# One decode step of a hybrid trunk: building the S5 input table with tokens and channels on partitions

## The chip, the cores and the metric

One core of a Trainium2 chip runs the whole kernel. The metric is the device time of one execution in microseconds (us), the median of three; the profile is one further execution. TensorE does the matrix products, VectorE and ScalarE the elementwise work, Pool (GpSimd) and SyncE mostly issue DMAs.

## The reference

Two layers over 256 prompt tokens and 8 samples of 4 tokens, 288 token columns in all, width 2048. Layer 0 mixes by retention and RG-LRU, layer 1 by S5, a diagonal complex state space model with 128 groups of 16 channels and 64 states; an FFN of 5632 follows each. The change touches only what S5 needs of its weights:

```python
def s5(u, h0_re, h0_im, a_re, a_im, b_re, b_im, c_re, c_im, d, log_dt):
    dt = jnp.exp(log_dt.astype(f32))[:, None]
    mag = jnp.exp(a_re * dt)
    abr = mag * jnp.cos(a_im * dt)
    abi = mag * jnp.sin(a_im * dt)
    ...
    bbr = fr[..., None] * b_re - fi[..., None] * b_im
    bbi = fr[..., None] * b_im + fi[..., None] * b_re
    ...
        _, _, sr, si = lax.associative_scan(_cplx_combine, (abr_c, abi_c, bu_r, bu_i), axis=1)
        y = jnp.einsum('bcgp,gkp->bcgk', sr, c_re) - jnp.einsum('bcgp,gkp->bcgk', si, c_im)
```

Both kernels work through the tokens in blocks of CH = 4. For a block they need, per pair of groups (32 channels, 128 states; 64 pairs), the complex input weights times the powers 3, 2, 1, 0 of the transition (table P), the output weights times the powers 1 to 4 (table O), the 4 x 4 token-to-token products (table T), and rotations for the scan over blocks (table R).

## The kernel before

Every weight matrix is streamed from DRAM in halves of up to 8 tiles of 128 x 128. For each half SyncE issues the load (`raw`, four buffers), ScalarE rounds it to `wh` (L268, four buffers) and VectorE forms the rest `wl = raw - wh` (L96); each tile then takes three matmuls of 288 columns (L314 to L316), 24 for a half of 8 tiles. Two halves make a unit, whose sum `acc` (two buffers) VectorE evacuates: in gate and up units into `g`, with the activation behind it, in down units as a residual add into `X`. The order on every engine is written out by the program, with no scheduler. After each half `run_prog` counts a step on and calls `run_due`, which runs what is due and then one piece of the queue `bgq`. Ahead of half s it has issued `wl` up to half s + 2:

```python
                if c[2] >= done + (4 if hold else 3) or c[2] >= n or c[2] in hold:
                    break
                prepl_next()
```

so on VectorE the order is: `wl` of half s + 2, evacuation after half s (every second half), the piece of `bgq`, `wl` of half s + 3, and so on. VectorE works in this order; what waits holds up all behind it.

The tables are built in the FFN of layer 0 by pieces of `bgq`: `t1` and `t2` (constants, four instructions a piece), then eight chunks of eight pairs of groups (`table_chunk`), 23 pieces each: 7 for the rotations, 4 for `bstep` (complex products of 128 columns, states on partitions, and copies by ScalarE into `pst`), 6 for `cstep`, 4 for `tp` and 2 for `tt_`. A piece `tp` transposes four 128 x 128 blocks of `pst` on TensorE (L1244), ScalarE scales them into `stg` (L1249), and after each second piece Pool writes 512 KB to the DRAM table `tabP` (L1252). A piece `tt_` does eight token products of 32 x 128, an fp32 product in two passes (L1261), and writes `tabT` and `tabO` from Pool (L1267, L1270). The last piece, `s5_open`, closes the tables' buffers and issues the first loads of the finished tables from SyncE, on the queue that also loads the weights.

## Time and profile before

| | |
|---|---|
| median of three runs | 2535.65 us (2535.18 to 2535.86) |
| span of the profiled execution | 2533.9 us |
| TensorE busy | 2468.4 us, 97% |
| VectorE busy | 1592.1 us, 63% |
| ScalarE busy | 1152.4 us, 45% |
| Pool busy, DMA issue not counted | 104.7 us, 4% |
| DMA | 468.31 MB, 185 GB/s in the mean |
| table build, first load to last table written | about 660 to 1265 us |

Busy time is the share of the span in which an engine had an instruction running. A wait in brackets is the idle time before an instruction and what ended it. Starts in a timeline count from the start of the span.

### The profile page before, as it was taken

To read this page: it belongs to the slowest core of one execution; us is meant where nothing else is said; L and a number is where in the kernel's file an instruction comes from. 1 tells how busy PE (TensorE), PEld (TensorE's weight loads), DVE (VectorE), ACT (ScalarE), POOL (GpSimd) and SP (SyncE) were. 2 spreads that over 40 slices of the span, in tenths; PEclk is the share of its full clock that TensorE was granted. 3 is DMA by queue.
4 is the path that set the end of the run, shared out by engine and by line. 5 is a ranking of instruction groups with operands and counts; after the bars stand their busy time and mean duration, and the time that the engine had idled before them with its cause. 6 is when DMAs were issued, how large, how long until landed. Compare 5 with 4: busy or idle time off the path is not lost.

```text
span 2533.9 us, 49270 instructions
## 1 busy us (share of the span) xinstructions
PE 2468.4 (97%) x20210; PEld 2428.2 (96%) x20210; DVE 1592.1 (63%) x2955; ACT 1152.4 (45%) x1786; POOL 104.7 (4%) x204
## 2 busy tenths in 40 slices
PE   8999999999999999999998789999999999999997
PEld 8899999999999999999997689999999999999997
DVE  7767666567766777667756975555544555445555
ACT  6646545433455655545533344443333333333342
POOL 0111110000000000000100000000000000000000
PEclk9999999999999999999999999999999999999999
DMA  7556645555566666666678855555455554445553
GB/s 251 181 173 193 203 151 181 164 166 167 182 217 198 209 199 207 212 210 196 204 239 250 277 163 165 167 164 166 164 163 173 166 164 161 161 163 166 167 163 125
DMA packets 155184, 468.31 MB, mean 185 GB/s; under 512 B 32912, under 2 KB 40976, under 8 KB 154960
## 3 DMA queue, kind: packets, MB, share of 16 engines
q1 hardware_dynamic: 140944, 421.16, 51.9%
q0 software_dynamic: 12288, 42.69, 4.6%
q8 instruction: 159, 2.61, 0.4%
q10 hardware_dynamic: 1728, 1.33, 0.2%
q14 instruction: 65, 0.53, 0.1%
HBM read 423.99 MB, written 41.11 MB: 184 GB/s over the span
## 4 chain that ended last, share of the span: by engine, by line
PE 92%; DVE 5%; DMA 2%; ACT 1%; issue 0%; SPq 0%; POOL 0%; DVEq 0%; ACTq 0%
PE acc L314 30%; PE acc L316 29%; PE acc L315 29%; DVE w L96 2%; DVE w L1421 1%; DMA raw<-in_w_in_dram 1%; PE mp L724 1%; PE mp L1244 1%; PE mp L776 0%; DVE Hs L96 0%; DVE g L105 0%; PE mp L1261 0%; PE mp L519 0%; DVE g L96 0%; DMA tab<-tabR 0%
## 5 line engine op out<-in xcount | busy, mean ns | idle before, releaser
L314 PE MATMUL acc<-xg,wh 128*128 128x288 f32 x3520 | 1047.9, 298 | 0.0
L268 ACT ACTIVATE wh<-raw 128x1024 fp32r<-128x1024 f32 (+1 forms) x736 | 758.9, 1035 | 426.2 <-PE acc L315 277.2
L316 PE MATMUL acc<-xg,wl 128*128 128x288 f32 x2816 | 829.0, 294 | 0.8 <-DVE wl L96 0.8
L315 PE MATMUL acc<-xg,wh 128*128 128x288 f32 x2608 | 765.5, 294 | 1.6 <-DVE xg L105 1.6
L96 DVE TENSOR_TENSOR wl<-raw,wh 128x1024 fp32r<-128x1024 f32 (+1 forms) x585 | 692.2, 1196 | 56.2 <-ACT wh L268 48.5
L314 PEld LDWEIGHTS acc<-xg,wh 128*128 128x128 f32 x3520 | 660.5, 188 | 3.0 <-issue 2.2
L314 PE MATMUL acc<-ac,wh 128*128 128x288 f32 x2064 | 613.5, 297 | 1.6 <-ACT ac L1479 1.0
L316 PEld LDWEIGHTS acc<-xg,wl 128*128 128x128 f32 x2816 | 529.2, 188 | 1.1 <-DVE wl L96 1.1
L315 PEld LDWEIGHTS acc<-xg,wh 128*128 128x128 f32 x2608 | 492.3, 189 | 2.5 <-DVE xg L105 2.0
L316 PE MATMUL acc<-ac,wl 128*128 128x288 f32 x1592 | 469.5, 295 | 0.7 <-DVE wl L96 0.7
L315 PE MATMUL acc<-ac,wh 128*128 128x288 f32 x1568 | 460.1, 293 | 0.0
L315 PE MATMUL acc<-x,wh 128*128 128x288 f32 x1408 | 415.4, 295 | 0.0
L314 PEld LDWEIGHTS acc<-ac,wh 128*128 128x128 f32 x2064 | 388.6, 188 | 4.7 <-issue 1.7
L96 DVE TENSOR_TENSOR g<-acc,rstd 128x288 f32<-128x288 f32 x192 | 87.6, 456 | 353.0 <-PE acc L316 352.5
L316 PEld LDWEIGHTS acc<-ac,wl 128*128 128x128 f32 x1592 | 300.0, 188 | 1.2 <-DVE wl L96 1.2
L315 PEld LDWEIGHTS acc<-ac,wh 128*128 128x128 f32 x1568 | 295.5, 188 | 0.0
L315 PEld LDWEIGHTS acc<-x,wh 128*128 128x128 f32 x1408 | 264.4, 188 | 0.1
L316 PE MATMUL acc<-xg,wlx 128*128 128x288 f32 x704 | 207.3, 294 | 0.0
L96 DVE TENSOR_TENSOR X<-X,acc 128x288 f32<-128x288 f32 x112 | 50.8, 454 | 243.2 <-PE acc L316 242.9
L96 DVE TENSOR_TENSOR wlx<-raw,wh 128x1024 fp32r<-128x1024 f32 (+1 forms) x151 | 179.4, 1188 | 6.8 <-ACT wh L268 6.8
L191 ACT ACTIVATE ac<-g 128x288 fp32r<-128x288 f32 x98 | 43.5, 444 | 286.9 <-DVE g L96 286.9
L316 PE MATMUL acc<-ac,wlx 128*128 128x288 f32 x472 | 139.2, 295 | 0.0
(279 smaller groups left out, 2030.3 us busy)
## 6 DMA issues: line engine op xcount, KB each, us to landing
raw<-in_w_gu_dram SPq DMA_DIRECT2D x352, 512.0 KB, 4.5
raw<-in_w_dn_dram SPq DMA_DIRECT2D x128, 448.0 KB, 4.1
raw<-in_w_in_dram SPq DMA_DIRECT2D x96, 512.0 KB, 4.5
raw<-in_w_dn_dram SPq DMA_DIRECT2D x64, 512.0 KB, 3.7
raw<-in_w_glu_dram SPq DMA_DIRECT2D x64, 512.0 KB, 4.7
raw<-in_w_out_dram SPq DMA_DIRECT2D x32, 512.0 KB, 4.4
out_ret_s_dram<-s POOLq DMA_DIRECT2D x16, 512.0 KB, 4.9
tabR<-R POOLq DMA_DIRECT2D x16, 512.0 KB, 6.8
```

What stands on the lines that cost most here:

```text
L96: v.tensor_tensor(o, a, b, op=op)
L191: act.activation(h, x, AF.Copy, scale=scale)
L268: act.activation(wh[:, :w], raws[i][:, :w], AF.Copy)
L314: pe.matmul(acc, lhsT=wh[:, o:o + P], rhs=xh, start=(k == u.k0), stop=False)
L315: pe.matmul(acc, lhsT=wh[:, o:o + P], rhs=xl, start=False, stop=False)
L316: pe.matmul(acc, lhsT=wl[:, o:o + P], rhs=xh, start=False, stop=(k == u.k1 - 1))
L724: pe.matmul(CR[h][32 * g:32 * g + 32, :256], lhsT=qm[:, dt, b2, :], rhs=t_[:, b2, dt, :], start=(c < 2 and dt == 0), stop=(c > 1 and dt == 1),
L1244: pe.transpose(ps[:, (2 * k + ri) * P:(2 * k + ri + 1) * P], st["ps"][:, ri, 4 * (jj // 2) + q].rearrange("p s i -> p (s i)"), ident)
L1421: v.tensor_tensor_scan(g[:, ri].rearrange("p q c -> p (q c)"), r4m, a[:, ri].rearrange("p q c -> p (q c)"), 0.0, op0=MUL, op1=ADD)
```

## The change

`t3` forms the input factor times the powers 0 to 3 for all groups in `s_wp` (states on partitions), `t4` transposes it in eight pieces and writes it to a new DRAM table `tabW`, 64 x 1024. A chunk then keeps one complex product of `bstep` (the power 0, for the token products). Table P is formed pair by pair with tokens and channels on partitions: for two pairs of groups (here called a pair, k = 0 to 3 in a chunk) `p_load` issues five DMAs from Pool, four that repeat a row of `tabW` over 32 partitions each (`pw`, 64 KB each) and one for the input weights, laid out ahead by the host (`pb`, 256 KB). `p_half` forms the real part in one piece and the imaginary part in the next, three VectorE operations of 256 columns each; the second of them also issues the next pair's loads, has ScalarE scale the result in place and Pool write 256 KB of `tabP`. `pw`, `pb` and `pout` have one buffer each. The sixteen token products of a chunk go into one PSUM bank in one piece. A chunk has 23 pieces as before: 7, 1, 6, 1 and 8.

```diff
     tabP = drp.tile([NT, P, 1024], F32, name="tabP")
     tabO = drp.tile([NT, P, 1024], F32, name="tabO")
     tabT = drp.tile([NT, P, P], F32, name="tabT")
+    tabW = drp.tile([64, CH, 2, P], F32, name="tabW")
     tabR = drp.tile([NT, P, 1024], F32, name="tabR")
...
-        later(10, lambda: (bgq.append(t1()), bgq.append(t2()), rest()))
+        wp = tb.tile([P, CH, 2, 64], F32, name="s_wp")
+
+        def t3():
+            for k, x in enumerate((fr, fi)):
+                v.tensor_copy(wp[:, 0, k], x)
+                yield 1
+            for e in range(1, CH):
+                pr, pi = wp[:, e - 1, 0], wp[:, e - 1, 1]
+                a, b, c, d = (g_(W) for _ in range(4))
+                tt(a, pr, abr, MUL)
+                yield 1
+                tt(b, pi, abi, MUL)
+                yield 1
+                tt(wp[:, e, 0], a, b, SUB)
+                yield 1
+                tt(c, pi, abr, MUL)
+                yield 1
+                tt(d, pr, abi, MUL)
+                yield 1
+                tt(wp[:, e, 1], c, d, ADD)
+                yield 1
+
+        def t4():
+            o = tb.tile([P, 2, 1024], F32, tag="R", name=nm("R"), bufs=1)[:64, 0]
+            for hf in range(2):
+                ps = mp_()
+                for k in range(4):
+                    pe.transpose(ps[:64, k * P:k * P + P], wp[:, 2 * hf + k // 2, k % 2], ident)
+                act.activation(o[:, 512 * hf:512 * hf + 512], ps[:64], AF.Copy)
+            pool.dma_start(tabW.rearrange("c e r n -> c (e r n)"), o)
+        later(10, lambda: (bgq.append(t1()), bgq.append(t2()), bgq.append(t3()), bgq.append(t4), rest()))
...
-            st["ps"] = tb.tile([P, 2, 8, CH, 32], F32, tag="ps", name=nm("pst"), bufs=1)
+            st["ps"] = tb.tile([P, 2, 8, 32], F32, tag="ps", name=nm("pst"), bufs=1)
...
-        def bput(e):
+        def bput():
             for ri in range(2):
-                put(st["ps"][:, ri, :, CH - 1 - e, :], st["w", e][ri], S["gm"])
+                put(st["ps"][:, ri], st["w"][ri], S["gm"])
...
-        def bstep(e):
-            def f():
-                if e == 0:
-                    b = st["bc"]
-                    st["w", 0] = cmul(bc(S["fr"]), bc(S["fi"]), b[:, :, 0], b[:, :, 1])
-                else:
-                    bput(e - 1)
-                    st["w", e] = cmul(bc(S["abr"]), bc(S["abi"]), *st["w", e - 1])
-            return f
+        def bstep():
+            b = st["bc"]
+            st["w"] = cmul(bc(S["fr"]), bc(S["fi"]), b[:, :, 0], b[:, :, 1])
...
-        def tp(jj):
+        def p_load(k):
+            c0 = 8 * ch + 2 * k
+            w = tb.tile([P, 2, 2, P], F32, tag="pw", name=nm("pw"), bufs=1)
+            b = tb.tile([P, 2, 2, P], F32, tag="pb", name=nm("pb"), bufs=1)
+            for s in range(CH):
+                pool.dma_start(w[32 * s:32 * s + 32], tabW[c0:c0 + 2, CH - 1 - s][None].to_broadcast([32, 2, 2, P]))
+            pool.dma_start(b, ins["ssm_bt"][:, c0:c0 + 2])
+            st["p", k] = w, b
+
+        def p_half(k, im):
             def f():
-                if jj % 2 == 0:
-                    st["stg"] = tb.tile([P, 4, 2, P], F32, tag="stg", name=nm("stg"), bufs=1)
-                ps = mp_()
-                for k in range(2):
-                    q = 2 * (jj % 2) + k
-                    for ri in range(2):
-                        pe.transpose(ps[:, (2 * k + ri) * P:(2 * k + ri + 1) * P],
-                                     st["ps"][:, ri, 4 * (jj // 2) + q].rearrange("p s i -> p (s i)"), ident)
-                for k in range(2):
-                    q = 2 * (jj % 2) + k
-                    c = 8 * ch + 4 * (jj // 2) + q
-                    act.activation(st["stg"][:, q].rearrange("p b c -> p (b c)"), ps[:, 256 * k:256 * k + 256],
-                                   AF.Copy, scale=S["g4"][:, c:c + 1])
-                if jj % 2:
-                    pool.dma_start(tabP[2 * ch + jj // 2], st["stg"].rearrange("p a b c -> p (a b c)"))
+                w, b = st["p", k]
+                if not im:
+                    st["po"] = tb.tile([P, 2, 2, P], F32, tag="po", name=nm("pout"), bufs=1)
+                x, y = (tb.tile([P, 2, P], F32, tag="px", name=nm("px"), bufs=2) for _ in range(2))
+                tt(x, w[:, :, 0], b[:, :, im], MUL)
+                tt(y, w[:, :, 1], b[:, :, 1 - im], MUL)
+                o = st["po"]
+                tt(o[:, :, im], x, y, ADD if im else SUB)
+                if im:
+                    if k < 3:
+                        p_load(k + 1)
+                    for q in range(2):
+                        c = 8 * ch + 2 * k + q
+                        act.activation(o[:, q], o[:, q], AF.Copy, scale=S["g4"][:, c:c + 1])
+                    pool.dma_start(tabP[c // 4][:, 512 * (k % 2):512 * (k % 2) + 512], o.rearrange("p q r n -> p (q r n)"))
             return f
 
-        def tt_(jj):
-            def f():
-                j = 2 * ch + jj
-                ps = mp_()
+        def tt_():
+            ps = mp_()
+            for jj in range(2):
                 for ri in range(2):
                     for q in range(4):
-                        pe.matmul(ps[32 * q:32 * q + 32, :P], lhsT=st["ps"][:, ri, 4 * jj + q, CH - 1, :],
+                        pe.matmul(ps[32 * q:32 * q + 32, P * jj:P * jj + P], lhsT=st["ps"][:, ri, 4 * jj + q, :],
                                   rhs=st["vz"][:, ri, 4 * jj + q, 0:CH, :].rearrange("p t o -> p (t o)"),
-                                  start=(ri == 0), stop=(ri == 1), tile_position=(0, 32 * q), skip_group_check=True)
+                                  start=(ri == 0 and jj == 0), stop=(ri == 1), tile_position=(0, 32 * q), skip_group_check=True)
+            for jj in range(2):
+                j = 2 * ch + jj
                 T = tb.tile([P, P], F32, tag="Tt", name=nm("Tt"), bufs=2)
-                act.activation(T, ps[:, :P], AF.Copy, scale=vec[:, V_ODD + j:V_ODD + j + 1])
+                act.activation(T, ps[:, P * jj:P * jj + P], AF.Copy, scale=vec[:, V_ODD + j:V_ODD + j + 1])
                 stt(T[:, :32], S["qm"], S["dg"][:, j:j + 1], T[:, :32], MUL, ADD)
                 pool.dma_start(tabT[j], T)
                 od = tabO[j].rearrange("p (q r n) -> p r q n", r=2, n=P)
                 for ri in range(2):
                     pool.dma_start(od[:, ri], st["vz"][:, ri, 4 * jj:4 * jj + 4, 1:CH + 1, :].rearrange("p q t o -> p q (t o)"))
-            return f
         def rview(c0, m0, m1):
...
-        for e in range(CH):
-            bgq.append(bstep(e))
+        bgq.append(bstep)
         for e in range(CH + 1):
             bgq.append(cstep(e))
-        bgq.append(lambda: cput(CH))
-        for jj in range(4):
-            bgq.append(tp(jj))
-        for jj in range(2):
-            bgq.append(tt_(jj))
+        bgq.append(lambda: (cput(CH), p_load(0)))
+        bgq.append(tt_)
+        for k in range(4):
+            bgq.append(p_half(k, 0))
+            bgq.append(p_half(k, 1))
...
+    bt = np.zeros((CH, 2, 16, 64, 2, 2, 64), np.float32)
+    for ri, k in enumerate(("ssm_b_re", "ssm_b_im")):
+        bg = a[k][0].reshape(64, 2, 64, 16).transpose(1, 3, 0, 2)
+        for g in range(2):
+            bt[:, g, :, :, ri, g, :] = bg[g]
+    o["ssm_bt"] = bt.reshape(P, 64, 2, P)
```

On Pool, from chunk 0's rotations (`tabR`) on, the queue before:

```order
L1303 DMA tabR<-R_7549 128x1024
L1252 DMA tabP<-stg_8249 128x1024 [waits Activation_49]
L1252 DMA tabP<-stg_8322 128x1024 [waits Activation_49]
L1267 DMA tabT<-Tt_8404 128x128 [waits DVE_49]
L1270 DMA tabO<-vzt_7548 512x1x128 x2
L1267 DMA tabT<-Tt_8449 128x128 [waits DVE_49]
L1270 DMA tabO<-vzt_7548 512x1x128 [waits DMASW2_49]
L1270 DMA tabO<-vzt_7548 512x1x128 [waits DMASW3_49]
```

and now, from the last token table of the chunk on (`DMASW` is the semaphore of a Pool DMA, `DMAHW` that of a SyncE DMA):

```order
L1305 DMA tabO<-vzt_7826 512x1x128 [waits DMASW6_49]
L1305 DMA tabO<-vzt_7826 512x1x128 [waits DMASW7_49]
L1266 DMA pw_8473<-tabW 32x2x256 [waits DMASW0_49,DVE_49]
L1266 DMA pw_8473<-tabW 32x2x256 [waits DMASW1_49]
L1266 DMA pw_8473<-tabW 32x2x256 [waits DMASW2_49]
L1266 DMA pw_8473<-tabW 32x2x256 [waits DMASW3_49]
L1267 DMA pb_8474<-in_ssm_bt_dram 128x512 [waits DMASW4_49]
L1286 DMA tabP<-pout_8435 128x512 [waits DMASW5_49,DVE_49,Activation_49]
L1266 DMA pw_8551<-tabW 32x2x256 [waits DMASW2_49,DMASW3_49,DMASW1_49,DMASW6_49,DMASW0_49,DVE_49]
```

Chunk 0's first loads (`pw_8342`, `pb_8343`) follow `tabR` directly and are not shown. The two large writes of `tabP` have become four smaller ones, and each but the last stands behind the five loads of the next pair, the first of which waits for VectorE.

On VectorE, in the same chunk, where the transposes and the token products stood, before:

```order
L96 TENSOR_TENSOR wl_117<-raw_8021,wh_8147 128x1024 [waits DMAHW3_49,Activation_49]
L96 TENSOR_TENSOR wl_115<-raw_8065,wh_8188 128x896 [waits DMAHW4_49,Activation_49]
L96 TENSOR_TENSOR X<-X,acc_8193 128x288 [waits PE_49]
L96 TENSOR_TENSOR wl_116<-raw_8106,wh_8222 128x1024 [waits DMAHW5_49,Activation_49]
L96 TENSOR_TENSOR wlx<-raw_8150,wh_8257 128x896 [waits DMAHW6_49,Activation_49]
L96 TENSOR_TENSOR X<-X,acc_8262 128x288 [waits PE_49]
L96 TENSOR_TENSOR wl_117<-raw_8191,wh_8295 128x1024 [waits DMAHW7_49,Activation_49]
L96 TENSOR_TENSOR wl_115<-raw_8225,wh_8330 128x896 [waits DMAHW0_49,Activation_49]
L96 TENSOR_TENSOR X<-X,acc_8335 128x288 [waits PE_49]
L105 SCALAR_TENSOR_TENSOR Tt_8404<-s_qm,s_dg,Tt_8404 128x32 [waits Activation_49]
```

and now:

```order
L96 TENSOR_TENSOR px_8468<-pw_8342,pb_8343 128x256 [waits DVE_49]
L96 TENSOR_TENSOR px_8469<-pw_8342,pb_8343 128x256
L96 TENSOR_TENSOR pout_8435<-px_8468,px_8469 128x2x128 [waits DVE_49]
L96 TENSOR_TENSOR wl_118<-raw_8311,wh_8441 128x1024 [waits DMAHW3_49,Activation_49]
L96 TENSOR_TENSOR px_8514<-pw_8473,pb_8474 128x256 [waits DMASW2_49,DMASW3_49,DMASW1_49,DMASW4_49,DMASW0_49,DVE_49]
L96 TENSOR_TENSOR px_8515<-pw_8473,pb_8474 128x256
L96 TENSOR_TENSOR pout_8513<-px_8514,px_8515 128x2x128 [waits DMASW5_49,DVE_49,Activation_49]
L96 TENSOR_TENSOR wl_116<-raw_8352,wh_8483 128x896 [waits DMAHW4_49,Activation_49]
L96 TENSOR_TENSOR X<-X,acc_8488 128x288 [waits PE_49]
L96 TENSOR_TENSOR px_8546<-pw_8473,pb_8474 128x256 [waits DVE_49]
```

Where only `wl` and `X` followed each other, each step now has three operations of a half, and the first half of the second pair waits for five Pool DMAs (its loads) and, at `pout`, for the write of the first pair.

On TensorE, one of the four places of a chunk where transposes stood between two halves, before:

```order
L315 MATMUL acc_8193<-ac_7927,wh_8103 128x288
L316 MATMUL acc_8193<-ac_7925,wlx 128x288
L1244 MATMUL mp_8250<-ident,pst_7547 128x128 x4
L314 MATMUL acc_8262<-ac_5814,wh_8147 128x288
L315 MATMUL acc_8262<-ac_5816,wh_8147 128x288
L316 MATMUL acc_8262<-ac_5814,wl_117 128x288
```

and the same chunk's token products now, where there were two groups of eight:

```order
L315 MATMUL acc_8313<-ac_7907,wh_8223 128x288
L316 MATMUL acc_8313<-ac_7905,wlx 128x288
L1294 MATMUL mp_8376<-vzt_7826,pst_7825 32x128 x16
L314 MATMUL acc_8410<-ac_5816,wh_8267 128x288
L315 MATMUL acc_8410<-ac_5818,wh_8267 128x288
L316 MATMUL acc_8410<-ac_5816,wl_118 128x288
```

The four transposes are gone from the chunk's first steps, and the sixteen products stand in one row of the queue.

## Rows read from the trace of the kernel before

**Rows 1.** The page: busy time by engine, and the chain's shares.

```profile
PE 2468.4 (97%) x20210; PEld 2428.2 (96%) x20210; DVE 1592.1 (63%) x2955; ACT 1152.4 (45%) x1786; POOL 104.7 (4%) x204
...
PE 92%; DVE 5%; DMA 2%; ACT 1%; issue 0%; SPq 0%; POOL 0%; DVEq 0%; ACTq 0%
```

**Rows 2.** Waits of TensorE: us in total, times, longest.

```profile
PE acc L316 <- DVE wl L96: 1.6, 3, 0.8
```

**Rows 3.** Stretches: us, each engine's busy time and instructions, PEclk, DMA share, GB/s.

```profile
600.00:620.00 20.00, 20.00 (x154) 20.00 (x153) 15.11 (x41) 7.38 (x9) 0.00 (x0) 1.00 0.46 149
...
1276.00:1286.00 10.00, 8.61 (x61) 7.91 (x61) 7.20 (x10) 5.84 (x8) 0.00 (x0) 1.00 0.64 198
...
1440.00:1460.00 20.00, 14.31 (x410) 12.59 (x402) 19.86 (x38) 9.01 (x23) 1.07 (x3) 0.86 0.91 266
```

**Rows 4.** Timeline (start us, us) of VectorE and SyncE near 1268.

```profile
1268.31 1.08 DVE L96 TENSOR_TENSOR wl<-raw,wh 128x896 fp32r<-128x896 f32 x1
1277.67 1.09 DVE L96 TENSOR_TENSOR wl<-raw,wh 128x896 fp32r<-128x896 f32 x1 [8.28 <-ACT wh L268]
...
1265.09 0.33 SPq L1356 DMA_DIRECT2D ss<-in_state_ssm_dram  x1
```

**Rows 5.** Timeline of TensorE around a group of transposes.

```profile
712.84 0.30 PE L316 MATMUL acc<-ac,wlx 128*128 128x288 f32 x1
712.98 0.60 PE L1244 MATMUL mp<-ident,pst 128*128 128x128 f32 x4
...
713.55 0.29 PE L315 MATMUL acc<-ac,wh 128*128 128x288 f32 x1
```

**Rows 6.** Groups by line: the transposes.

```profile
L1244 PE MATMUL mp<-ident,pst 128*128 128x128 f32 x128 | 19.2, 272 | 0.0
```

**Rows 7.** Timeline of TensorE around a group of token products.

```profile
726.60 0.29 PE L316 MATMUL acc<-ac,wlx 128*128 128x288 f32 x1
726.82 0.65 PE L1261 MATMUL mp<-vzt,pst 128*32 128x128 f32 x16
...
727.63 0.29 PE L315 MATMUL acc<-ac,wh 128*128 128x288 f32 x1
```

**Rows 8.** Timeline of VectorE: weights, 256-column operations, evacuation.

```profile
709.06 2.22 DVE L96 TENSOR_TENSOR wl<-raw,wh 128x1024 fp32r<-128x1024 f32 x2
...
749.07 1.42 DVE L96 TENSOR_TENSOR rt<-R,s_pw 128x256 f32<-128x256 f32 x4
750.41 0.75 DVE L96 TENSOR_TENSOR R<-rt,rt 128x256 f32<-128x256 f32 x2
...
803.24 0.46 DVE L96 TENSOR_TENSOR g<-acc,rstd 128x288 f32<-128x288 f32 x1 [1.42 <-PE acc L316]
...
805.44 0.25 DVE L105 SCALAR_TENSOR_TENSOR Tt<-s_qm,s_dg,Tt 128x32 f32<-128x32 f32 x1
```

**Rows 9.** Timeline of Pool: DMAs being issued.

```profile
729.02 1.51 POOL L1270 DMA_DIRECT2D tabO<-vzt  x2
...
753.89 1.09 POOL L1303 DMA_DIRECT2D tabR<-R  x2 [19.41 <-ACT wh L268]
```

**Rows 10.** DMA issues: times, KB each, median us to landing.

```profile
...
tabP<-stg POOLq DMA_DIRECT2D x16, 512.0 KB, 5.9
tabO<-vzt POOLq DMA_DIRECT2D x32, 256.0 KB, 6.1
out_ret_p_dram<-so POOLq DMA_DIRECT2D x4, 256.0 KB, 2.4
tabT<-Tt POOLq DMA_DIRECT2D x16, 64.0 KB, 4.1
```

**Rows 11.** The tile `stg`: its engine's waits, who waited, landing.

```profile
  DMA tabP<-stg: 28.6, 7
...
  PEld acc L314: 0.2, 1
...
DMA to landing us min/median/max: 3.4/5.9/6.7
```

More of the change, by code (lines that the diff above doesn't have):

```diff
@@ L1228, in f @@
                 if e == 0:
-                    bput(CH - 1)
+                    bput()
                     st["c", 0] = (st["bc"][:, :, 2], st["bc"][:, :, 3])
```

## The prediction

> **What bounds the kernel now.** Read the page's busy line and chain first [rows 1]: TensorE is busy for 97% of the span and holds 92% of the chain, so time taken off it is gained in full as long as nothing makes it wait. The waits of TensorE say how near that is: in the whole run it waited 1.6 us for a prepared weight `wl` [rows 2]. The stretches place the table build: it lies inside layer 0's FFN, where TensorE is busy 20.00 of 20 us with 154 matmuls at clock 1.00 [rows 3], or 0.13 us each. A weight half is thus 24 x 0.13 = 3.1 us in gate/up, and 22.5 x 0.13 = 2.9 us on average in the down projection (15 tiles a unit). I call that a step; one piece of the background queue goes with each.
>
> What keeps TensorE fed is that VectorE's subtraction `wl` is written three steps ahead. How far that carries is seen once [rows 4]: VectorE stood still for 8.28 us between two of these subtractions, and in the ten us in which that reached TensorE it was busy 8.61 [rows 3], so 1.39 us was lost. A single stop of about 7 us is free; two in a row are not, unless there is time to catch up between them.
>
> **The change part by part.**
>
> *TensorE.* A group of four transposes sits between a matmul that starts at 712.84 and one that starts at 713.55 [rows 5]: 0.71 us, less two ordinary spacings (0.26), is 0.45. There are 128 transposes, 32 groups [rows 6]: 32 x 0.45 = 14.4 us go. A group of eight token products takes 1.03 - 0.26 = 0.77 us [rows 7], of which its 16 passes after the first take (0.65 - 0.27) / 15 = 0.025 each. One group of sixteen products then costs 0.77 + 16 x 0.025 = 1.17 in place of 1.54: 8 x 0.37 = 3.0 us go (between 0 and 6, as all or nothing of a group is fixed cost). The eight new transposes of the powers come at most at the price of the old ones, 2 x 0.45, and I take 0.8. TensorE alone: -14.4 - 3.0 + 0.8 = -16.6 us.
>
> *Position.* The powers put seven pieces into the queue; a chunk still has 23. All chunks come seven steps (some 20 us) later, still within the FFN. I count nothing for that, except at the end (below). `tabW` leaves through the `R` buffer, which chunk 0 wants back one step later: one stop of a landing, within the cover; I take 1 us.
>
> *VectorE and ScalarE work.* Per chunk three complex products of 128 columns go (18 instructions) and eight halves of 256 columns come (three each). Four independent operations of 256 columns start within 1.34 us (749.07 to 750.41), 0.33 each, and the third of a half waits for the second, about 0.45 [rows 8]: a half takes 0.33 + 0.45 + 0.33 = 1.1 us. Eight a chunk are 8.8 us; the 18 operations saved are of half the width, so each costs between half of 0.33 and 0.33, 3 to 6 us. VectorE has 24 to 46 us more in all, in time in which it is idle now. ScalarE loses 96 copies. None of it is on TensorE's path by itself.
>
> *The new waits.* This is the term that decides. The powers `pw`, the input weights `pb` and the output `po` have one buffer each. The second half of pair k releases `pw` and `pb` when its second product has read them, 0.4 us before its end. Only then can Pool issue the five DMAs of pair k+1, and the order shows VectorE's next product, one step later, waiting for all five. Pool needs 1.09 us for two and 1.51 us for two of the finer ones [rows 9], so 0.53 each: the last, `pb` (256 KB), is issued 4 x 0.53 - 0.4 = 1.7 us after the half's end. Call its time to landing L. The first half of pair k+1 then ends 1.7 + L + 1.1 = 2.8 + L after the second half of pair k. `po` comes free at nearly the same time: `tabP` is issued sixth, 2.2 us after the half, and lands L later, while the first half wants to write it at 2.5 + L. Behind the waiting product VectorE has the next `wl`, the evacuation of an accumulator and the second half queued, and TensorE waits for that `wl`.
>
> From one second half to the next it takes (2.8 + L) + 1.1 for a `wl` (two in 2.22 us, [rows 8]) + 1.1 for the half itself + e = 5.0 + L + e, and in this time TensorE gets two weights. e is the evacuation where it falls between the two halves: the order shows it there in chunks 0 and 4 (residual add, 0.4) and in chunks 2 and 6 (gate and up: 0.4 and, 803.24 to 805.44, 2.2, mean 1.3 [rows 8]); in the odd chunks it is hidden in the wait (0).
>
> L is not shown for a reload, so it is bounded by Pool's other DMAs [rows 10]: 2.4 us for 256 KB of `out_ret_p`, issued in the even mixer, and medians of 4.1, 5.9 and 6.1 for `tabT`, `tabP` and `tabO` in this very stretch, with single ones of 3.4 to 6.7 [rows 11]. The reload is 256 KB behind four of 64 KB, beside the same weight loads: nearest to the three of this stretch. I take 5.0, ends 2.4 and 6.5.
>
> By the Trainium skill ("DMA: Bandwidth & Descriptors", Anatomy of one DMA) a DMA issued from GpSimd costs about 2.0 us and its bytes at 436 KB per us. That would be 2.6 us here, close to the even mixer's 2.4, while the FFN's rows lie twice as high. By that page the change would come out near the second rival's time.
>
> With L = 5.0 the period is 10.0, 10.4 and 11.3 us, against two steps of 6.3, 5.9 and 6.3: 3.7, 4.5 and 5.0 us too long. The first wait of a chunk still has cover. In an even chunk the evacuation at time 0 is followed by e and a half (1.1), then 2.8 + L and a `wl`: at 10.0 + e the `wl` is there that TensorE wants at three steps, so it is 10.4 - 8.8 = 1.6 late with the residual add, 11.3 - 9.4 = 1.9 in gate/up. In an odd chunk it is there at 1.3 + 1.1 + 1.1 + 1.1 + 8.9 = 13.5, wanted at four steps, 12.6: 0.9 late. Pair 0's load is issued a dozen steps early and costs nothing. So a chunk loses its first lateness and two excesses: odd 0.9 + 7.4 = 8.3, chunks 0 and 4 1.6 + 9.0 = 10.6, chunks 2 and 6 1.9 + 10.0 = 11.9. Four, two and two of them: 33 + 21 + 24 = 78 us.
>
> *The end of the build.* `s5_open` follows the last piece on the same DMA queue as the weights and waits for the last table to be written (1265.09, [rows 4]); that made the 8.28 us stop. Afterwards the blocking is no longer than that, but TensorE comes to it with no weights ahead: between 0 and 8 us more, I take 4.
>
> **Sum.** -16.6 + 1 + 78 + 4 = +66 us. The profiled span is 2533.9 us and 1.75 us lie around it up to the median of 2535.65, so 2600.3 + 1.75 = 2602 us.
>
> **The rivals.**
>
> *The reload lands quickly (same).* Place: VectorE's wait for `pb`. With L = 2.4 the excesses are 1.1, 1.9 and 2.4, the first waits are 1.7, 1.0 and 0.7 within cover; chunks lose 0.5, 2.8 and 4.1, together 2 + 5.6 + 8.2 = 16 us, which is the gain on TensorE: 2533 to 2540 us. For it: `out_ret_p`, and that slower weights mean fewer weight loads beside the reload. Against: every median of this stretch.
>
> *The wait is covered altogether (faster).* `stg` has the same kind of single buffer now: ScalarE waited 28.6 us for `tabP` in seven cases, and TensorE waited 0.2 us for that group [rows 11]. If VectorE's wait is as harmless, 2535.65 - 16.6 = 2519 us. What decides is whether the period fits in two steps, L up to 1.3 us in odd chunks; no DMA of Pool does that. ScalarE's seven waits are spread over eight chunks, and VectorE would wait three times running in each, with a `wl` behind every wait.
>
> *The clock falls as well (slower still).* In the S5 stretch, where TensorE is busy 14.31 of 20 us, the granted clock is 0.86 [rows 3], so in part 1.2 GHz. The starved part of a chunk is some 30 us with TensorE busy 6 of 10. At 0.89 over 8 x 30 us that is 26 us: 2628 us. Against: the half speed mostly falls into time in which TensorE waits anyway, and the one gap now (1276 to 1286) kept 1.00.
>
> **How the numbers follow.** Forecast 72%, with 2560 (L = 3.4: chunks lose 3.5, 5.8, 7.0, together 40 us, less 16.6 and no end term) to 2650 (L = 6.5: 114 us and 8 at the end) as its own ends; quick reload 12%; covered 3%; clock 13%. About 0.2%, 5 us, is what a measurement here can tell from no change. Faster: 3% and a third of the quick reload, 7%. Same: the other 8%. Slower: 85%. The range leaves out the two quick cases (15%) below and a few per cent above: 2545 to 2648.
>
> **What would show it.** Right: no transposes between the FFN's matmuls but for eight; VectorE idle before `px` and `pout` three times a chunk for some 4 to 6 us each, put down to DMAs into `pw` or `pb` or out of `pout`; TensorE waiting for `wl` in eight clusters, together some 80 us, and at 100% elsewhere in the FFN; the span of the other layers unchanged. Wrong: `pb` landing 2 to 3 us after issue (then same), or VectorE's waits there with TensorE still at 20.00 of 20 us (then the cover is deeper than I read it, and 2519 stands).

## Result and profile after

The changed kernel takes 2644.06 us (median of 4, 2641.6 to 2645.93) against 2535.76 us (2535.18 to 2537.29) for the kernel before, measured side by side: ratio 1.0429, 95% interval 1.0416 to 1.0441. The prediction was 2602 us (2545 to 2648): the direction and the place are as it said, and the loss is 108 us instead of 66.

The page of the changed kernel, busy time by engine and the shares of the chain (compare [rows 1]):

```profile
PE 2492.4 (94%) x20090; PEld 2449.7 (93%) x20090; DVE 1632.5 (62%) x3023; ACT 1127.2 (43%) x1692; POOL 202.1 (8%) x381
...
PE 81%; DVE 9%; DMA 7%; POOL 2%; issue 1%; ACT 1%; DVEq 0%; SPq 0%; ACTq 0%; POOLq 0%
```

The profiled span is 2639.8 us, 105.9 more than before. TensorE has 120 instructions fewer and is still busy 24.0 us longer; its idle time in the span rises from 2533.9 - 2468.4 = 65.5 to 147.4, by 81.9. The two make 105.9. The chain, 92% TensorE before, now runs through VectorE, DMAs and Pool for 18% (7% before). Pool's busy time, of which the table of the kernel before says that issuing is not counted, does contain its DMA issues: 71 of the 105 us before, 175 of the 202 us now.

Where it happens is shown by the first matmul after the table build, S5's `po`. One row of each kernel, before and then after, from the view of the tile `X` (min, median and max ns, first and last start in us):

```profile
L1437 PE MATMUL po<-X,ones x32: 406/406/849, 1367.5 to 1395.9; 128*128 128x288 f32 x32
```

```profile
L1470 PE MATMUL po<-X,ones x32: 406/406/849, 1473.4 to 1501.8; 128*128 128x288 f32 x32
```

It starts 105.9 us later, and from it to the end both kernels take 1166.4 us. The whole loss lies in layer 0's FFN, with the chunks.

Waits in the changed kernel (us in total, times, longest us), first TensorE's, to be held against the 1.6 us of [rows 2], then VectorE's on a reload:

```profile
PE acc L316 <- DVE wl L96: 58.5, 20, 5.2
PE acc L316 <- DVE wlx L96: 25.4, 6, 4.9
...
DVE px L96 <- DMA pb<-in_ssm_bt_dram: 140.8, 24, 7.7
```

24 waits of VectorE are three in each of eight chunks, one for each reloaded pair. One pair of chunk 0 shows the chain: the timeline of VectorE (start us, us, what ended the idle time before), then of Pool:

```profile
733.43 0.43 DVE L96 TENSOR_TENSOR pout<-px,px 128x256 f32<-128x256 f32 x1
733.78 1.22 DVE L96 TENSOR_TENSOR wl<-raw,wh 128x1024 fp32r<-128x1024 f32 x1
741.13 0.76 DVE L96 TENSOR_TENSOR px<-pw,pb 128x256 f32<-128x256 f32 x2 [6.13 <-DMA pb<-in_ssm_bt_dram]
741.98 0.43 DVE L96 TENSOR_TENSOR pout<-px,px 128x256 f32<-128x256 f32 x1
742.32 1.08 DVE L96 TENSOR_TENSOR wl<-raw,wh 128x896 fp32r<-128x896 f32 x1
743.33 0.45 DVE L96 TENSOR_TENSOR X<-X,acc 128x288 f32<-128x288 f32 x1
743.69 0.75 DVE L96 TENSOR_TENSOR px<-pw,pb 128x256 f32<-128x256 f32 x2
744.48 0.42 DVE L96 TENSOR_TENSOR pout<-px,px 128x256 f32<-128x256 f32 x1
```

```profile
733.69 2.15 POOL L1266 DMA_DIRECT2D pw<-tabW  x4 [2.50 <-DVE px L96]
735.83 0.61 POOL L1267 DMA_DIRECT2D pb<-in_ssm_bt_dram  x1
736.44 0.56 POOL L1286 DMA_DIRECT2D tabP<-pout  x1
```

The second half of pair 0 ends at 733.86. Pool may issue from 733.69 and spends 2.15 us on the four transfers of `pw`; `pb` goes out at 735.83, 2.0 us after the half (the prediction: 1.7), and VectorE goes on at 741.13, 5.3 us after that. From one second half to the next it is 744.48 - 733.43 = 11.05 us, and 11.2 and 11.7 for the next two, with two `wl` in each. TensorE uses up two `wl` in 5.9 us here (two steps of the down projection).

What that does to TensorE is in its own timeline and in stretches (us, each engine's busy time and instructions, PEclk, DMA share, GB/s) of the same chunk:

```profile
743.46 0.40 PE L316 MATMUL acc<-ac,wl 128*128 128x288 f32 x1 [1.84 <-DVE wl L96]
754.64 0.61 PE L316 MATMUL acc<-ac,wlx 128*128 128x288 f32 x1 [3.42 <-DVE wlx L96]
766.39 0.61 PE L316 MATMUL acc<-ac,wl 128*128 128x288 f32 x1 [4.14 <-DVE wl L96]
```

```profile
744.00:747.00 3.00, 3.00 (x15) 3.00 (x15) 2.01 (x4) 2.01 (x4) 2.26 (x5) 0.52 0.70 195
748.00:751.00 3.00, 3.00 (x25) 2.99 (x23) 0.00 (x0) 0.00 (x0) 0.04 (x1) 1.00 0.89 306
```

Three waits: 1.84, 3.42 and 4.14 us. After the first, the granted clock is at 1.2 GHz (0.52, nearly all of the stretch) though TensorE is busy all the time: 15 matmuls start in 3 us, and 25 in 3 us a little later, at 2.4 GHz. With 20 of the 24 stops of 1.5 us and more in this FFN the clock falls like this, behind the stop or within it; before there were no such stops.

The landings (times, KB each, median us from issue to landing; compare [rows 10]):

```profile
pw<-tabW POOLq DMA_DIRECT2D x128, 64.0 KB, 5.1
pb<-in_ssm_bt_dram POOLq DMA_DIRECT2D x32, 256.0 KB, 6.0
tabP<-pout POOLq DMA_DIRECT2D x32, 256.0 KB, 5.7
```

These medians are not yet the prediction's L. Eight of the 32 `pb` are the first loads of a chunk; they land after 8.5 to 10.1 us, and nothing waits for them. The 24 reloads, for which VectorE waits, land after 4.2 to 6.7 us, 5.6 in the mean (6.0 in the odd chunks, 5.3 in the even ones). The prediction took 5.0. In chunk 0, the first load (issues from 706 to 707 us) and then the three reloads (725 to 765 us):

```profile
pb<-in_ssm_bt_dram POOLq DMA_DIRECT2D x1, 256.0 KB, 8.7
...
pb<-in_ssm_bt_dram POOLq DMA_DIRECT2D x3, 256.0 KB, 5.2
```

### The profile page after: what moved, and what is told of

Same layout as the page of the kernel before. It is cut to its first block, busy times and chain, and to the rows that moved or that the text cites. A ratio compares the mean times of both kernels' runs of the same rounds, so it can differ in the third digit from the quotient of the medians.

```text
span 2639.8 us, 49372 instructions
## 1 busy us (share of the span) xinstructions
PE 2492.4 (94%) x20090; PEld 2449.7 (93%) x20090; DVE 1632.5 (62%) x3023; ACT 1127.2 (43%) x1692; POOL 202.1 (8%) x381
## 4 chain that ended last, share of the span: by engine, by line
PE 81%; DVE 9%; DMA 7%; POOL 2%; issue 1%; ACT 1%; DVEq 0%; SPq 0%; ACTq 0%; POOLq 0%
PE acc L314 26%; PE acc L316 26%; PE acc L315 26%; DMA pb<-in_ssm_bt_dram 5%; DVE w L96 2%; POOL pw L1266 2%; DVE wl L96 1%; DVE px L96 1%; DVE w L1454 1%; DMA raw<-in_w_in_dram 1%; PE mp L724 1%; DVE g L96 1%; DVE g L105 0%; DVE wlx L96 0%; PE mp L776 0%
## 5 line engine op out<-in xcount | busy, mean ns | idle before, releaser
L316 PE MATMUL acc<-xg,wl 128*128 128x288 f32 x2816 | 837.4, 297 | 38.5 <-DVE wl L96 38.5
L314 PEld LDWEIGHTS acc<-xg,wh 128*128 128x128 f32 x3520 | 670.7, 191 | 1.8 <-issue 1.2
L316 PEld LDWEIGHTS acc<-xg,wl 128*128 128x128 f32 x2816 | 536.6, 191 | 41.6 <-DVE wl L96 41.6
L315 PEld LDWEIGHTS acc<-xg,wh 128*128 128x128 f32 x2608 | 501.6, 192 | 2.0 <-DVE xg L105 1.4
L314 PEld LDWEIGHTS acc<-ac,wh 128*128 128x128 f32 x2064 | 393.7, 191 | 4.9 <-ACT ac L1512 2.4
L315 PEld LDWEIGHTS acc<-ac,wh 128*128 128x128 f32 x1568 | 300.6, 192 | 0.0
L316 PEld LDWEIGHTS acc<-xg,wlx 128*128 128x128 f32 x704 | 135.4, 192 | 18.9 <-DVE wlx L96 18.9
```

The lines of the kernel that those rows point to most:

```text
L314: pe.matmul(acc, lhsT=wh[:, o:o + P], rhs=xh, start=(k == u.k0), stop=False)
L315: pe.matmul(acc, lhsT=wh[:, o:o + P], rhs=xl, start=False, stop=False)
L316: pe.matmul(acc, lhsT=wl[:, o:o + P], rhs=xh, start=False, stop=(k == u.k1 - 1))
```

## Experiments

Ratios are to runs of the kernel before, taken beside them on the same chip (medians 2534.7 to 2535.0 us). Theory: VectorE's waits on the single buffers starve TensorE, and nothing else does. The rivals: it is the larger VectorE work, the DMA traffic, or the clock.

### The same work, not in a row

Between a pair and the next stand two pieces of the next chunk's rotations (`front`; empty pieces behind the last chunk):

```diff
-        for k in range(4):
-            bgq.append(p_half(k, 0))
-            bgq.append(p_half(k, 1))
...
+            for k in range(4):
+                bgq.extend(halves[2 * k:2 * k + 2])
+                if k < 3:
+                    bgq.extend(front[:2])
+                    front = front[2:]
```

> The changed kernel with the same instructions, buffers and DMAs, in another order: two pieces of the next chunk's rotations stand between the second half of a pair and the first half of the next (nothing but empty pieces after the last chunk). Theory (the single-buffered reload, 9 us from half to half, does not fit in two steps): with four steps of 2.9 to 3.1 us it fits, VectorE's waits for pb fall from 141 us to under 40, TensorE's for wl from 84 to under 5, time 2519 to 2526 us. Rival (the added work itself costs it: 32 x 512 KB of DMA, 36 us of VectorE): waits move but the time stays above 2600.

Measured 2526.91 us, ratio 0.9968 (0.9957 to 0.9979), 0.9 us above the range that was expected. VectorE's waits (us, times, longest):

```profile
DVE px L96 <- DMA pb<-in_ssm_bt_dram: 12.7, 7, 3.7
```

The landing is no quicker (median 6.2 us), the instructions, bytes and buffers are the same, and the half-speed stretches among the chunks are gone; one is left in the FFN, behind a stop 13 us after `s5_open` (columns as above):

```profile
1305.00:1308.00 3.00, 3.00 (x14) 3.00 (x14) 2.35 (x4) 1.54 (x4) 0.00 (x0) 0.50 1.09 349
```

So 117 of the changed kernel's microseconds hang on the order alone: two steps more between the pairs give the reload the time that it needs. More VectorE work and more traffic are excluded as causes by themselves.

### Two buffers, one side of the wait and both

For the loads alone, issued two pairs ahead (room is made by letting temporaries share buffers):

```diff
-            w = tb.tile([P, 2, 2, P], F32, tag="pw", name=nm("pw"), bufs=1)
-            b = tb.tile([P, 2, 2, P], F32, tag="pb", name=nm("pb"), bufs=1)
+            w = tb.tile([P, 2, 2, P], F32, tag="pw", name=nm("pw"), bufs=2)
+            b = tb.tile([P, 2, 2, P], F32, tag="pb", name=nm("pb"), bufs=2)
...
-                    if k < 3:
-                        p_load(k + 1)
+                    if k < 2:
+                        p_load(k + 2)
...
```

> As with two buffers each, but pout keeps its one buffer. Theory of two waits of nearly equal length: tabP is issued behind the five loads, 2.4 us after the second half, lands 5.7 us later, so the next first half ends 8.5 us after the second half instead of 8.9: 24 x 0.4 us better only, 2620 to 2640 us, with VectorE now waiting for tabP at pout. Rival (only the reload matters): 2519 to 2526 us.

Measured 2618.44 us, ratio 1.033 (1.0315 to 1.0344), 1.6 us below the range of the theory and far from the rival. The 24 waits have moved one instruction on, from the load's landing to the store's:

```profile
DVE pout L96 <- DMA tabP<-pout: 127.0, 24, 8.0
```

and `pout` too with two buffers:

```diff
-                    st["po"] = tb.tile([P, 2, 2, P], F32, tag="po", name=nm("pout"), bufs=1)
+                    st["po"] = tb.tile([P, 2, 2, P], F32, tag="po", name=nm("pout"), bufs=2)
```

> The changed kernel with two buffers each for pw, pb and pout, the loads of a pair issued two pairs ahead; room is made by letting s_wp and px use other tags' buffers and by 8 instead of 10 buffers of td. Theory: same as for the order change, 2519 to 2526 us. Rival (order and work cost it): above 2600.

Measured 2523.72 us, ratio 0.9955 (0.9942 to 0.9969). TensorE's waits for `wl` are 2.1 us in all, and its busy time shows what the change takes off it when nothing starves:

```profile
PE 2451.2 (97%) x20090; PEld 2413.3 (96%) x20090; DVE 1632.0 (65%) x3023; ACT 1126.8 (45%) x1692; POOL 201.4 (8%) x381
```

2468.4 - 2451.2 = 17.2 us. Of 120 us that two buffers for everything bring, two for the loads bring 26. That is more than the 24 x 0.4 = 10 us of the theory: before the last round of each chunk no loads are issued there any more, and that store goes out 1.3 us after the half and not 2.6, 8 x 1.3 = 10 us more; the last 6 are not attributed. In the changed kernel the store's wait can hardly be seen (VectorE waited 1.1 us for it, once), because the store lands just before it is asked for: 8.3 us after the half in the mean of the 24 rounds, while VectorE, released by the load at 7.8, wants to write at 8.6.

### The reload left out

```diff
-                w, b = st["p", k]
+                w, b = st["p", 0]
...
-                    if k < 3:
-                        p_load(k + 1)
```

> Leaves out the reloads of pw and pb for the second to fourth pair of each chunk: these pairs are computed from the first pair's weights and inputs, so part of the table is wrong; instructions on VectorE and the store of each pair are those of the changed kernel. Theory (two waits lie behind each other in a period, and with the reload gone the store of pout, which has one buffer, sets it): the store is issued about 1.1 us after the pair and lands 5.7 us later, so a period is about 9.5 us and not 11.4, 24 x 1.9 = 46 us less: 2595 to 2620 us. Rival (the reload is the only cause): 2519 to 2526, as with the pairs spread out.

Measured 2585.29 us, ratio 1.0197 (1.0182 to 1.0213): below the theory's 2595, far above the rival's 2526.

```profile
DVE pout L96 <- DMA tabP<-pout: 88.8, 24, 4.8
```

That the store goes out earlier was in the expectation (1.1 us after the half; measured 1.3). What it had not is that it also lands sooner: with the reload gone, 5.0 us in the median instead of 5.7, and 4.8 in the mean of the 24 that are waited for. From one second half to the next it is 9.2 us in the mean, where the changed kernel has 11.6: 24 x 2.4 = 57 of the 59 us gained. The single output buffer by itself still costs some 60 us over 2524.

### The token products alone

The kernel before, with only the token-to-token products of all 16 pairs in one group:

```diff
-        for jj in range(2):
-            bgq.append(tt_(jj))
+        bgq.append(tt_)
```

> The kernel before with the token products in one group of sixteen and nothing else changed. Theory: 8 x 0.37 us of TensorE less, 2533 us, ratio 0.9988. Rivals: nothing (2535.8), or the whole fixed part of a group, 8 x 0.77 = 6 us (2529.6).

Measured 2532.74 us against 2534.9, ratio 0.9992 (0.9983 to 1.0001). TensorE's busy time falls by 3.6 us (2464.8 for 2468.4), 3.0 being the prediction's term; the time agrees with it, but the interval holds no change as well.

### How much of it is the clock

```diff
+        def keep():
+            ps = mp_()
+            for _ in range(6):
+                pe.matmul(ps[:, :N], lhsT=ones, rhs=X[:, 0, :], start=True, stop=True, skip_group_check=True)
...
+                if im == 0 and k > 1:
+                    keep()
...
```

> Changed kernel plus six matmuls of 288 columns, whose result nothing reads, after the first half of each chunk's third and fourth pair and at the next chunk's load: 18 x 7 + 12 = 138 matmuls of about 0.48 us, 66 us of TensorE's time put into stretches where it waits. Question: what the stretches at half clock (92 us in all in the FFN, 41 us more busy time on TensorE) cost by themselves. Theory (the stretches fall where TensorE would have waited anyway for the two thirds, so the clock's own share of the loss is 16 to 20 us): 2624 to 2632 us if the clock stays at full level, with fewer stretches at 1.2 GHz. Rival 1 (the clock costs nothing by itself, since TensorE waits for VectorE then): 2644 or more, up to 2670 where the added matmuls push work. Rival 2 (the clock's whole 41 us lie on the path): about 2603.

Measured 2637.43 us, ratio 1.0406 (1.039 to 1.0422), 6.6 us below the changed kernel and 5 above the upper end of what was expected. The two intervals just overlap (the changed kernel has 1.0416 to 1.0441). The stretch of the FFN in the changed kernel and in this one (columns as above), then the group of the added matmuls (busy us, mean ns of one):

```profile
600.00:1380.00 780.00, 701.04 (x5202) 692.57 (x5200) 517.16 (x1240) 330.45 (x562) 146.62 (x256) 0.95 0.63 196
```

```profile
600.00:1380.00 780.00, 747.08 (x5519) 724.75 (x5518) 524.33 (x1251) 333.81 (x568) 146.69 (x257) 0.99 0.63 198
```

```profile
L1273 PE MATMUL mp<-X,ones 128*128 128x288 f32 x276 | 70.7, 406 | 0.0
```

The clock goes from 0.95 to 0.99 and TensorE does 70.7 us more, and yet VectorE's waits (138.8 us, 24 times) and nearly all of the loss stay. In the changed kernel busy time that the clock cost is 2492.4 - 2451.2 = 41.2 us. But a matmul slowed before another wait of the same chunk only shortens that wait, since VectorE's chain doesn't depend on it. What counts is half speed after the last wait of a chunk: read in stretches of half a microsecond, the eight chunks lost 2.5, 0, 1.5, 1.7, 1.7, 1.7, 2.0 and 3.0 there, together 14 us. The expectation of 16 to 20 had taken a flat share of two thirds as harmless.

In the kernel with the added matmuls 5.1 us of the 14 remained (chunks 2, 5 and 7), so by this reading 9 us should come back. The place of the same matmuls in both traces shows 11.3 us gained over the eight chunks, of which the rounds, 11.50 us in the mean for 11.63, explain some 24 x 0.13 = 3; single chunks differ from the reading by up to 2 us. Behind the build 4.1 us were lost again: TensorE stopped after `s5_open` for 3.1 us in place of 1.3, and ran at half speed behind that. So the 6.6 us are not the clock's share alone, and the 14 us stay a reading of the trace that this run fits and does not prove.

### The four weight transfers

If issuing were what delays `pb`, one transfer for `pw` in place of four should help.

```diff
-            for s in range(CH):
-                pool.dma_start(w[32 * s:32 * s + 32], tabW[c0:c0 + 2, CH - 1 - s][None].to_broadcast([32, 2, 2, P]))
+            pool.dma_start(w.rearrange("p c r n -> p c (r n)"), tabW[:, c0:c0 + 2][:, None].to_broadcast([CH, 32, 2, 256]))
...
```

> The table of weights in device memory is stored by power, so that the four transfers of a pair's weights become one of the same bytes, and pw and pb are two issues on GpSimd's queue in place of five. In the changed kernel the four take 2.15 us of GpSimd's time (about 0.54 each) before pb's starts, and pb is the last to land. Theory (the reload's serial chain, issue and landing, is what the two halves wait for): one issue in place of four shortens each of 24 periods by some 1.6 us, 24 x 1.6 = 38 us, of which the stretches at half clock may give back a little more: 2600 to 2610 us. Rival 1 (the landing is slow because 16 queues are busy with the weights of the FFN, and the issue is covered): no change, 2640 us. Rival 2 (what makes the landing long is the burst of five transfers at once): more than the issue comes back, the landing falls from 6.0 to some 4 us, and the time goes to 2560 to 2590.

Measured 2689.12 us, ratio 1.0604 (1.0586 to 1.0622), 45 us slower than the changed kernel, against every theory. The issue was as short as expected (0.71 us for 2.15), but the landings grew:

```profile
pw<-tabW POOLq DMA_DIRECT2D x32, 256.0 KB, 9.0
pb<-in_ssm_bt_dram POOLq DMA_DIRECT2D x32, 256.0 KB, 9.0
tabP<-pout POOLq DMA_DIRECT2D x32, 256.0 KB, 8.1
```

The packets of the whole run, in the changed kernel and here:

```profile
DMA packets 162178, 485.37 MB, mean 184 GB/s; under 512 B 35744, under 2 KB 43808, under 8 KB 161952
```

```profile
DMA packets 166785, 485.40 MB, mean 181 GB/s; under 512 B 40352, under 2 KB 48416, under 8 KB 166560
```

The same data go in 4608 more packets, all under 512 bytes, 144 for each merged transfer. The medians hold the chunks' first loads; of the 24 reloads `pb` landed after 8.3 us in the mean, where the changed kernel has 5.6, and the last of the two transfers 9.0 us after the half and not 7.6. This kernel also stores the table the other way round, so that edit was run with four transfers:

```diff
-    tabW = drp.tile([64, CH, 2, P], F32, name="tabW")
+    tabW = drp.tile([CH, 64, 2 * P], F32, name="tabW")
...
```

> Takes one of the two edits of the kernel with one transfer of weights: the table of weights in device memory is stored by power, but the four transfers of a pair stay four. Question: why the single transfer of the same 256 KB made the landings of pw and pb longer (medians 9.0 and 9.0 us against 5.1 and 6.0) and the kernel 45 us slower. Theory (it is the shape of the merged transfer, which shows 144 more small packets each): with four transfers the landings are back at 5 and 6 us and the time at 2640 to 2648. Rival (it is the order of the table in device memory): landings stay near 9 us and the time near 2689.

Measured 2645.84 us, ratio 1.0436 (1.0421 to 1.0452); `pw` and `pb` land in 5.1 and 6.0 us, to the digit those of the changed kernel. So it is the merged shape. A rule of the Trainium skill would fit ("DMA: Bandwidth & Descriptors", Why a DMA increments its semaphore by 16 and not by 1): a transfer is spread over the largest number of engines, at most 16, that divides the outermost size of both patterns, with an exception for some copies issued from GpSimd. As the kernels write them, that size is 32 on both sides of each of the four, and 4 at the source of the merged one. The packets in the trace carry no engine, but their sizes would suit four: each merged transfer shows 64 packets of 4 KB, 4 x 16, and 192 of 8 bytes, 12 x 16, that no other transfer has (and 48 of 4 bytes less than the four together). No run here shows how many engines a transfer used, so this cause stays argued.

With `pb` issued ahead of `pw`:

```diff
+            pool.dma_start(b, ins["ssm_bt"][:, c0:c0 + 2])
             for s in range(CH):
...
-            pool.dma_start(b, ins["ssm_bt"][:, c0:c0 + 2])
```

> Changed kernel with the 256 KB of pb issued ahead of the four transfers of pw, not behind them: same transfers, same queue. Theory (each transfer takes its own time from its issue, so the last of the five to be issued decides): the last is now one of 64 KB, median 5.1 us to landing in place of 6.0, at about the same issue time: 24 x 0.9 = 22 us less, 2615 to 2630. Rival (the transfers of the queue are served in order, so that the whole 512 KB behind the first issue decides): no change, 2640 to 2648.

Measured 2648.75 us, ratio 1.0447 (1.043 to 1.0465): no gain. The two medians change places:

```profile
pb<-in_ssm_bt_dram POOLq DMA_DIRECT2D x32, 256.0 KB, 5.1
pw<-tabW POOLq DMA_DIRECT2D x128, 64.0 KB, 5.6
```

and VectorE now waits for `pw`, 144.2 us in 24 times. In the 24 reloads the transfer that is issued last lands 5.7 us after its issue in the mean, here the fourth of `pw`, where it was 5.6 with `pb`; from the first issue to the last landing it is 7.9 us, where it was 7.8. VectorE waits for what is issued last, and a transfer of a quarter of the size in that place brings no gain: the time came out as the rival had it.

### Both cures at once

The edits of the two kernels above, two buffers for `pw`, `pb` and `pout` and the pairs spread out:

```diff
-                    if k < 3:
-                        p_load(k + 1)
+                    if k < 2:
+                        p_load(k + 2)
...
+                bgq.extend(halves[2 * k:2 * k + 2])
+                if k < 3:
+                    bgq.extend(front[:2])
+                    front = front[2:]
```

> Both cures at once: two buffers for pw, pb and pout with loads two pairs ahead, and two pieces of the next chunk's rotations between the pairs. Theory (with two buffers no wait of the pairs is left that TensorE sees; the spread one has 4.6 us of waits for the first FFN weight product, the one with two buffers none): the time stays at that of two buffers alone, 2520 to 2525 us. Rival (residual waits on VectorE still delay the end of the build): 2515 to 2519.

Measured 2520.41 us, ratio 0.9942 (0.9927 to 0.9956): the fastest version here and in the range of the theory, though its interval overlaps that of two buffers alone. `po` starts at 1352.0, 15.5 us earlier than before the change. What is still lost in the FFN lies behind `s5_open`: TensorE stops for 2.4 us there (4.3 with two buffers alone, 1.2 in the kernel before), and the clock is at 1.2 GHz for some 3 us behind it.

## Why the prediction was right, and where its sizes were off

**The work on TensorE** was sized well: -16.6 us predicted, 17.2 us less busy time with two buffers, and 2520.41 us for the best version, where the rival of a covered wait had 2519. The stop at `tabW` was one wait of 3.3 us on VectorE that no wait of TensorE answers; its term of +1 was 0. VectorE's work rose by 40.4 us (24 to 46 predicted) and cost nothing by itself, as the run with the pairs spread out shows.

**The new waits** are the mechanism that decided, with the count (three a chunk), the place and the order of waits foretold. Their size was too small. TensorE's idle time grew by 81.9 us, and about 27 of the 41 us of the clock (see there) lie in time that would have been waited: 109 us at full clock, where the sum had 78. The term that was mis-sized is the period from one second half to the next, here from the starts of `pout` in VectorE's timeline:

| chunks | predicted, us | measured, mean, us |
|---|---|---|
| odd | 10.0 | 11.6 |
| 0 and 4 | 10.4 | 10.9 |
| 2 and 6 | 11.3 | 12.4 |
| the 24 rounds | 10.4 | 11.6 |

Each round is 1.2 us longer, 24 x 1.2 = 29 us, and 78 + 29 = 107. Half of the 1.2 is L, 5.6 for 5.0. A quarter is the issue of `pb`, 2.0 us after the half and not 1.7: Pool starts only 0.29 us after the product that releases the buffers has ended, which the sum put at nothing. (Its 0.53 us for one issue is not quite what its rows give, 1.09 / 2 = 0.545; measured 0.54.) From the landing to the product it is 0.15 us more. The lateness at a chunk's first wait agrees in chunk 0 (1.6 predicted, 1.84 measured) and not in all: the eight together are 23.4 us for 10.6, of which the longer period explains 8 x 1.2. As for L, the row nearest to the reload was `tabO`, 256 KB of the same stretch in [rows 10], with 6.1; the prediction went below it towards the quicker ones.

By the Trainium skill ("DMA: Bandwidth & Descriptors", Anatomy of one DMA) an estimate of L is 2.6 us, close to the quick reload's 2.4, and the change would be about neutral; that is the time of the first rival, and not of the second, as the prediction has it. The measured 4.2 to 6.7 us contradict it for this place, a burst of five transfers beside the weight loads.

**The clock** was written as a rival, in place of the forecast; it came on top of it. The row on which it was discounted, one gap with PEclk 1.00 in [rows 3], had 1.39 us of idle time, most of it in two stops of 0.6; the new stops are of 1.6 to 5.2 us. Its reason, that half speed falls mostly into time that is waited anyway, was right for 27 of 41 us by the reading above. The other 14 us were missing from the sum.

**The end of the build** (+4) was 0 in the changed kernel: TensorE stops there once, for 1.3 us, and before it was 0.6 twice.

```profile
1277.69 0.40 PE L314 MATMUL acc<-ac,wh 128*128 128x288 f32 x1 [0.64 <-ACT wh L268]
1278.81 0.40 PE L316 MATMUL acc<-ac,wl 128*128 128x288 f32 x1 [0.59 <-DVE wl L96]
```

So by the same steps: -17 + 0 + 107 + 14 + 0 = +104 of the 106 us in the spans. The 2 us left are not attributed.

**The range** held with some luck. Its upper end was built on 2650 us for L = 6.5, but the terms given for it, 2535.65 - 16.6 + 1 + 114 + 8, make 2642. The measured 2644.06 us lie above that worst case, with L at 5.6: the clock (14 us) and 24 x 0.6 = 14 us of the period that are not L stand in for the longer landing.

**The store behind the load** was named in the prediction (`tabP` sixth in the queue, `pout` wanted at nearly the same time), and it decided what a cure is worth: two buffers for the loads alone brought 26 us of 120, and the reload left out 59.

## What to carry to other kernels

Before a producer with single buffers is put in a row on an engine that also feeds TensorE, add up issue, landing and use of one round, and compare that period with the time in which TensorE uses what the engine delivers in it; the shares of busy time tell nothing of it. Take the landing from transfers of the same stretch and size, of those alone that are waited for, and expect a load and a store that wait in parallel to replace one another: both need a second buffer, or two other steps between the rounds. After a stop of TensorE, look at the granted clock too, and count only what is slow behind the last wait.

## What was not expected of the hardware

- One transfer that replicates four rows onto 128 partitions took 9.0 us to land in the median, where four of a quarter took 5.1 each, with the same bytes, and those behind it on Pool's queue landed later too (`pb` 9.0 for 6.0, `tabP` 8.1 for 5.7).
- The granted clock fell to 1.2 GHz for 3 to 7 us with 20 of 24 stops of TensorE in the FFN; the four without it were of 1.6 to 2.1 us, the shortest with it 1.84. With the pairs spread out, the waits for `wl` among the chunks were 0.8 us at most, and none was followed by it; the one fall there came behind two stops of 2.5 and 1.3 us.
- Behind 256 KB and three of its like on Pool's queue a transfer of 64 KB takes as long to land (5.7 us in the mean of 24) as one of 256 KB behind four of 64 (5.6), and the issue of either occupies Pool for 0.54 to 0.60 us.
- A chunk's first `pb` took 8.5 to 10.1 us, the reloads of the same size 4.2 to 6.7; no run here was made to tell why.
